# Low parts of the weights: all 861 subtractions on VectorE, and the MLP's second square on ScalarE

## The chip, the core and the metric

The kernel runs on one core of a Trainium2 chip. The metric is device microseconds of one execution. Engines are named as in the profile: PE is TensorE (PEld its weight loads), DVE is VectorE, ACT is ScalarE, POOL is GpSimd, SP is SyncE.

## What is computed

A forward pass of 256 tokens of width 1024 through two blocks of two layers each, in float32. The first block has latent attention, memory cross attention, an MLP, stick-breaking attention, again cross attention and an MLP. The second has retention, a layer of experts, sparse attention (nsa) and a second layer of experts, with scales and shifts from a conditioning vector (adaLN). What matters here:

```python
def sq_relu_mlp(h, w_in, w_out):
    return jnp.square(jax.nn.relu(h @ w_in)) @ w_out

def peer(h, w_q, sub_keys, u_tab, v_tab):
    ...
        s = jnp.einsum('thcd,hcnd->thcn', q, sub_keys, preferred_element_type=f32)
        sv, si = lax.top_k(s, PEER_TOPK)
    ...
        cv, ci = lax.top_k(comb, PEER_TOPK)
    ...
        w = jax.nn.softmax(cv, axis=-1)
        u = u_tab[eidx]
        a = jax.nn.gelu(jnp.einsum('td,thkd->thk', xc, u, preferred_element_type=f32)) * w
        return jnp.einsum('thk,thkd->td', a.astype(v_tab.dtype), v_tab[eidx])
```

The tables u and v hold 16384 experts. The kernel doesn't gather them: it multiplies with all of them and weights the result by masks.

## The kernel before

**Weights in two parts.** Every product is made of three: high part times high part, and the two mixed products with the low parts, all in float32r. The weights come as a stream of 861 granules of 128 x 1024 float32 (512 KB), in the order of use. For each granule SP loads `raw`, ACT copies it rounded to float32r into `wh` (L279), and a subtraction makes `wl` = `raw` - `wh` (L285). There are four buffers of each. A granule serves 24 matmuls of 256 columns or 12 of 512.

**The order around it.** Nothing is scheduled by a tool; each engine runs what the program issues, in that order. `block()` hands out the weights. At the first block of a granule it runs one step of each background generator (`tick`), then `ahead()`, then the posts. `ahead()` first issues the subtraction of the granule cast one granule earlier, and with it the load that refills its raw buffer, then casts the granule three places further on. So a low part is issued two granules before its use. In `_conv` the engine of the subtraction is chosen by a counter:

```python
        eng = k.nc.gpsimd if k.pool_share and (g + 1) % k.pool_share == 0 else k.nc.vector
```

With `pool_share` 2 every second granule goes to POOL, with 1 each, with 3 each third, with 0 none; it is 2 for most stages and is set anew around some of them. At 1 it stands where DVE builds masks.

**The MLP** (`mlp`, L1087 to L1114). Each of the 32 tiles of the hidden layer takes one granule. Behind it ACT makes z = relu (L1100) and the high part of z squared (L1101), DVE squares z again in full float32 (L1102) and subtracts (L1103). Through these stages the adaLN vector is made in the background: of every three steps of `ada_gen` two issue a load of 512 KB and a DVE reduction of 128 x 1024 (L697).

**The expert layers** (`peer`). While PE makes queries and the first products with u, DVE searches the 16 largest scores of 32 rows, later of 16 more (`top16`, L1504 to L1512). The generator `route` takes two searches where the cast counter is even and one where it is odd (L1551). Then masks are made: L1607 on DVE, L1611 on POOL, sums L1618 and L1619 on DVE. Each product tile of u is added up by DVE (L1683). In four stages `w_gen` weights the hidden values by masks E, A and B on DVE (L1700, L1702, L1705), which PE multiplies (L1713), and DVE scales (L1720). The products with v (L1769) take their operand from a split whose low part gl is made on DVE (L555).

**Other work named.** A split (L557, L558) makes high and low halves of an operand (`x`, `raw`, `m`); sums of squares are added up on POOL (L349).

Of the kernel before, what the change touches and what calls it, by code (L numbers as in the profile page):

```python
# [19 lines left out]
S = 256  # L20
# [27 lines left out]
# ---------------------------------------------------------------- host layout  # L48


def _tiles(w, cols):
    """Blocks [128, 128] of w[K, N] for the column tiles in cols, K innermost."""
    k = w.shape[0] // P
    out = []
    for c in cols:
        t = w[:, c].reshape(k, P, P)
        out.append(t)
    return np.concatenate(out, axis=0)


def _grans(blocks):
    """[n, 128, c] blocks to granules [g, 128, 1024]."""
# [8 lines left out]
def _pack_t(w, cols=None, group=0):  # L71
    """Column tiles one after another; the first group of them block by block in turn."""
# [10 lines left out]
def _pack_v(w, width=512):  # L83
    """Blocks [128, width], column group outermost, K innermost."""
    k, n = w.shape[0] // P, w.shape[1] // width
    b = w.reshape(k, P, n, width).transpose(2, 0, 1, 3).reshape(n * k, P, width)
    return _grans(b)


def _feat(v):  # L90
    """[..., n * 128] vectors to columns [128, ...]."""
    return np.ascontiguousarray(v).reshape(-1, P).T
# [47 lines left out]
def _rope_cols():  # L140
    """Per row of the table: frequency, phase, phase in turns."""
# [101 lines left out]
# ---------------------------------------------------------------- weight stream  # L243


class Stream:
    """Weights in order of use: loaded ahead, then split into a float32r part and its rest."""
# [25 lines left out]
    def _conv(self):  # L273
# [6 lines left out]
        eng = k.nc.gpsimd if k.pool_share and (g + 1) % k.pool_share == 0 else k.nc.vector  # L280
# [3 lines left out]
        def rest():  # L284
            eng.tensor_tensor(l, raw, h.bitcast(F32), op=ALU.subtract)  # L285
# [9 lines left out]
    def ahead(self):  # L295
        """Casts go AHEAD granules in front, their rests one turn later, when the cast is done."""
# [30 lines left out]
# ---------------------------------------------------------------- kernel body  # L327


class TileSum:  # L330
    """Sums over the features of n tiles: all but the last add up on another engine, then ones times both."""
# [34 lines left out]
class Kern:  # L366
    def __init__(self, tc, aps, ctx):
# [6 lines left out]
        self.pool_share = 2  # L374
        self.mk, self.mst, self.mv = [], [], []

    # -- helpers
# [15 lines left out]
    def logexp(self):  # L393
        """Ln and Exp from one table set."""
        self.nc.scalar.preload_act_table_set("natural_log_exp_and_others")

    def post(self, f):
        """Run f, which waits for another engine, behind what can go first."""
        self.posts.append(f)
# [6 lines left out]
    def later(self, f, tiles=1):  # L406
        """Run f, work for the tensor engine, so many product tiles later."""
        self.defer.append([tiles, f])

    def due(self, cap=3):  # L410
        """What to run behind the tile that starts now."""
# [27 lines left out]
    def pair(self, pool, name, kts=KT):  # L439
        """Tiles of an operand and of its rest, side by side: both, and the two as one."""  # L440
# [3 lines left out]
    def lin_head(self, name, xh, xl, kt, evac, psum, tag, pre=None, look=5, hook=None, banks=None, ahead=False):  # L444
        """The first GROUP tiles of a product at once, so that each operand tile serves them all when it comes.
        banks: one for each, for operands wider than S."""
# [39 lines left out]
    def lin_t(self, name, xh, xl, kt, nt, evac, psum=None, tag="lin", first=0, mid=32, hook=None, hl=None):  # L486
        """out^T tiles [128, S] of (x @ w): weights stationary.
        hl: the operand and its rest side by side, for tiles that take both with one load of the weights; the last tile doesn't."""
# [30 lines left out]
    def lin_v(self, name, xh, xl, kt, cg, evac, pre=None, look=3, mid=KT, hook=None):  # L519
        """out tiles [128 tokens, 512] of (x @ w): activations stationary."""  # L520
# [28 lines left out]
    def split(self, h, l, src, scale=None):  # L549
        """h + l = src (* scale per partition), both float32r."""  # L550
# [9 lines left out]
    def rstd(self, ps, n, eps, pool, name, width=S, out=None):  # L560
        """(ps / n + eps) ** -0.5 with one Newton step."""
# [26 lines left out]
    # -- setup  # L588
# [16 lines left out]
    def early_load(self, u):  # L605
        """The rest of the first loads, between the first units of weights."""
# [18 lines left out]
    def bank(self, kind, shape):  # L625
        """A bank for short use: in turn from those of all kinds, or from its own kind's."""
# [12 lines left out]
    def rope_table(self, room):  # L639
        """Rows of cosines, then sines with the signs that the swapped halves take."""  # L640
# [27 lines left out]
    def silu_c(self):  # L668
        """c / (1 + exp(-c)), by exponentials and a logarithm"""
# [13 lines left out]
    def ada_gen(self):  # L683
        """mod[:, j] = sum_k silu(c)[k] * w[k, j * 128 + p] + bias, one tile of features per step."""
# [22 lines left out]
    # -- residual stream with an RMS norm ahead  # L707

    def norm_begin(self, gname, gi, kts=KT, tag="x", pool=None, bank="sum"):
        """Operands of x * g; the norm's factor per token comes later from finish()."""  # L710
# [19 lines left out]
    def resid(self, name, oh, ol, kt, nxt, scale=None, pre=None, hl=None):  # L730
        """X += o @ w, tile by tile, with the next norm's operands."""
# [17 lines left out]
        if pre:  # L749
            share, self.pool_share = self.pool_share, 1 if kt < KT else self.pool_share  # L750
            self.lin_head(name, oh, ol, kt, evac, self.ps, "lin", pre=pre, look=1)
            self.pool_share = share
        self.lin_t(name, oh, ol, kt, KT, evac, first=GROUP if pre else 0, hl=hl)

    def late(self, st, n, name, flush=True):
        """The norm's factor, worked out behind the first product that uses the operands."""
# [8 lines left out]
    # -- softmax attention  # L765

    def soft_causal(self, ps, scale, pool, sb=3):
        """Rows of [q0 x k0 | q1 x (k0, k1)] in ps; exponentials and their sums, for soft_norm."""
# [38 lines left out]
    def pv(self, pT, v0, v1):  # L807
        """o^T [dv, q] from [k0 x (q0, q1) | k1 x q1]."""
# [6 lines left out]
    class Pipe:  # L815
        """Steps of heads; step i + 1 of a head comes lag[i] turns after step i."""
# [24 lines left out]
        def pre(self, every, head=lambda e: e):  # L841
            """Hook of lin_head: the heads left over come out while the products that need them last go on."""
# [12 lines left out]
    # -- block 1  # L855

    def mla(self):
# [3 lines left out]
        with tc.tile_pool(name="mla", bufs=1, reuse_waits="tile") as mp:  # L861
# [19 lines left out]
            def lat_norms(n):  # L881
                """Factors of the two inner norms on top of the outer one."""
# [26 lines left out]
            share, self.pool_share = self.pool_share, 3  # L909
            self.lin_head("mla_dkv", st["h"], st["l"], KT, evac, self.ps, "lin", pre=pre, look=KT)  # L910
            self.pool_share = share
# [1313 lines left out]
```

## Time and profile before

| what | value |
|---|---|
| median of 3 runs | 3097.62 us |
| the runs | 3095.78, 3097.62, 3098.09 us |
| span of the profiled execution | 3094.6 us, 46975 instructions |
| time of the profiled execution itself | not given apart from its span; the runs lie 1.2 to 3.5 us above the span, the median 3.0 |
| PE / DVE / ACT / POOL busy | 94% / 72% / 47% / 48% |
| subtractions on POOL / on DVE | 496 / 365 |

Busy time is the union of an engine's instructions; the mean of a group is over its single durations, which overlap slightly where instructions follow each other. "Idle before" names what ended the idle time of an engine. A wait is put down to the releaser that came last.

### The profile page before, as it was taken

The numbers are of one execution on the slowest core, as the hardware profiler recorded it, in microseconds if no ns is written. First come the engines' busy times: TensorE is split into PE (matmuls) and PEld (weight loads), VectorE is DVE, ScalarE is ACT, GpSimd is POOL, SyncE is SP. The second block draws the span as 40 slices with busy tenths as digits, with TensorE's granted clock in tenths as the row PEclk, the third lists the DMA queues.
The fourth block names the chain that finished last, engine by engine and source line by source line (L and its number), as shares of the span: only waits on it lengthen the run. The fifth ranks groups of instructions, "written<-read, shape, count | busy, mean of one in ns | idle before, by whom it ended". The sixth has DMA issues, their size and how long they took to land.

```text
span 3094.6 us, 46975 instructions
## 1 busy us (share of the span) xinstructions
PE 2920.4 (94%) x17758; PEld 2566.3 (83%) x17758; DVE 2218.5 (72%) x3966; ACT 1467.0 (47%) x2347; POOL 1500.5 (48%) x758
## 2 busy tenths in 40 slices
PE   7898999889999899999999999788999999999998
PEld 6888888888988887898888888677988898888886
DVE  6869986799768898676547666787897773367434
ACT  6455444553544555434542344565555334532444
POOL 4344456435555556454444444423566444455443
PEclk9999999999999999999999999999999999999999
DMA  5547775477554455434653356332455335643463
GB/s 180 197 152 253 283 271 207 164 266 287 183 177 130 146 182 166 145 112 140 188 170 109 123 188 188 117 110 77 157 184 177 124 113 171 186 145 114 150 188 119
DMA packets 143408, 521.06 MB, mean 168 GB/s; under 512 B 15919, under 2 KB 17229, under 8 KB 142669
## 3 DMA queue, kind: packets, MB, share of 16 engines
q1 hardware_dynamic: 142893, 515.96, 50.4%
q8 instruction: 139, 2.28, 0.3%
q10 hardware_dynamic: 288, 2.10, 0.2%
q14 instruction: 88, 0.72, 0.1%
HBM read 516.95 MB, written 1.05 MB: 167 GB/s over the span
## 4 chain that ended last, share of the span: by engine, by line
PE 64%; DVE 24%; issue 5%; POOL 3%; ACT 3%; DMA 1%; SPq 0%; DVEq 0%; ACTq 0%; POOLq 0%
PE vo L1769 22%; PE u L1675 11%; PE w L1713 8%; PE u L1676 6%; DVE wl L285 5%; DVE adaw L697 2%; PE lin L499 2%; PE lin L437 2%; PE lin L435 2%; DVE y L1102 2%; PE lin L436 2%; POOL wl L285 1%; PE lin L500 1%; POOL oh L1611 1%; PE lin L539 1%
## 5 line engine op out<-in xcount | busy, mean ns | idle before, releaser
L285 POOL TENSOR_TENSOR wl<-raw,wh 128x1024 fp32r<-128x1024 f32 x496 | 1248.1, 2518 | 1350.6 <-ACT wh L279 1340.5
L279 ACT ACTIVATE wh<-raw 128x1024 fp32r<-128x1024 f32 x861 | 910.3, 1058 | 650.6 <-PE vo L1769 331.6
L1675 PE MATMUL u<-x,wh 128*128 128x512 f32 x2048 | 731.8, 400 | 0.0
L285 DVE TENSOR_TENSOR wl<-raw,wh 128x1024 fp32r<-128x1024 f32 x365 | 557.1, 1527 | 227.7 <-ACT wh L279 227.5
L1676 PE MATMUL u<-x,wl 128*128 128x256 f32 x2048 | 577.5, 282 | 16.7 <-POOL wl L285 8.5
L1675 PEld LDWEIGHTS u<-x,wh 128*128 128x128 f32 x2048 | 387.8, 189 | 87.6
L1676 PEld LDWEIGHTS u<-x,wl 128*128 128x128 f32 x2048 | 389.0, 190 | 23.8 <-POOL wl L285 12.0
L1769 PE MATMUL vo<-wh,gh 128*128 128x512 f32 x1008 | 322.3, 401 | 0.0
L1769 PE MATMUL vo<-wh,gl 128*128 128x512 f32 x1008 | 316.3, 395 | 0.0
L1769 PE MATMUL vo<-wl,gh 128*128 128x512 f32 x1008 | 316.1, 395 | 0.0
L437 PE MATMUL lin<-x,wl 128*128 128x256 f32 x920 | 267.9, 291 | 24.3 <-DVE wl L285 22.3
L1713 PE MATMUL w<-B,A 128*128 128x64 f16 x2048 | 274.6, 303 | 9.7 <-DVE B L1705 9.5
L435 PE MATMUL lin<-x,wh 128*128 128x256 f32 x920 | 274.1, 298 | 3.3 <-DVE cq L558 2.8
L1713 PEld LDWEIGHTS <-A 128*128 128x128 f16 x2048 | 240.6, 147 | 38.2 <-DVE A L1702 19.9
L436 PE MATMUL lin<-x,wh 128*128 128x256 f32 x920 | 264.7, 288 | 3.6 <-DVE x L558 3.6
L1680 ACT COPY G<-u 128x256 f32<-128x256 f32 x256 | 94.8, 370 | 335.7 <-PE u L1676 335.1
L555 DVE TENSOR_TENSOR gl<-G,gh 128x512 fp32r<-128x512 f32 x128 | 170.7, 1334 | 93.5 <-ACT gh L554 93.3
L1769 PEld LDWEIGHTS vo<-wl,gh 128*128 128x128 f32 x1008 | 190.2, 189 | 44.6
L1769 PEld LDWEIGHTS vo<-wh,gl 128*128 128x128 f32 x1008 | 190.1, 189 | 44.3
L1769 PEld LDWEIGHTS vo<-wh,gh 128*128 128x128 f32 x1008 | 186.7, 191 | 38.8
L1683 DVE TENSOR_TENSOR G<-u,G 128x256 f32<-128x256 f32 x256 | 106.4, 417 | 149.7 <-ACT G L1680 149.6
L437 PEld LDWEIGHTS lin<-x,wl 128*128 128x128 f32 x920 | 180.2, 196 | 31.3 <-DVE wl L285 28.1
(551 smaller groups left out, 5471.0 us busy)
## 6 DMA issues: line engine op xcount, KB each, us to landing
raw<-in_peer_u SPq DMA_DIRECT2D x256, 512.0 KB, 3.5
raw<-in_peer_v SPq DMA_DIRECT2D x256, 512.0 KB, 3.6
adaw<-in_ada SPq DMA_DIRECT2D x112, 512.0 KB, 5.2
raw<-in_mlp_in SPq DMA_DIRECT2D x64, 512.0 KB, 4.5
raw<-in_mlp_out SPq DMA_DIRECT2D x64, 512.0 KB, 5.0
raw<-in_peer_q SPq DMA_DIRECT2D x32, 512.0 KB, 3.5
raw<-in_sb_qk SPq DMA_DIRECT2D x16, 512.0 KB, 4.3
raw<-in_ret_g SPq DMA_DIRECT2D x16, 512.0 KB, 3.6
```

The lines of the kernel that those rows point to most:

```text
L279: k.nc.scalar.activation(h, raw, AF.Copy)
L285: eng.tensor_tensor(l, raw, h.bitcast(F32), op=ALU.subtract)
L435: mm(ps, wh, xh, start=start, stop=False)
L436: mm(ps, wh, xl, start=False, stop=False)
L437: mm(ps, wl, xh, start=False, stop=stop)
L555: self.post(lambda: vec.tensor_tensor(l, src, h.bitcast(F32), op=ALU.subtract))
L1675: mm(p, wh, hx[:, i], start=i == 0, stop=False, skip_group_check=True)
L1676: mm(p[:, 0, :], wl, hh[:, i, :], start=False, stop=i == KT - 1, skip_group_check=True)
L1680: nc.scalar.copy(g, p[:, 1, :])
L1683: nc.vector.tensor_tensor(g, p[:, 0, :], g, op=ALU.add)
L1713: mm(pt[:, t, :], A[:, :, t], B[:, j, :, t], start=j == 0, stop=j == 1)
L1769: mm(vo[2 * b + e], x[:, j, t], w[:, e * 512:(e + 1) * 512], start=fst and m == 0, stop=bool(lst) and m == 2)
```

## The change

All subtractions are issued on DVE, and `pool_share` with every place that sets it is gone. In the MLP, the full square of z is made by ACT, by a Square activation. Comments and doc strings are gone as well, which shifts the line numbers (L285 is L284 after, L1683 is L1676).

```diff
@@ -277,12 +277,11 @@
         k.nc.scalar.activation(h, raw, AF.Copy)
-        eng = k.nc.gpsimd if k.pool_share and (g + 1) % k.pool_share == 0 else k.nc.vector
         self.conv[g] = (h, l)
         self.next_conv += 1

         def rest():
-            eng.tensor_tensor(l, raw, h.bitcast(F32), op=ALU.subtract)
+            k.nc.vector.tensor_tensor(l, raw, h.bitcast(F32), op=ALU.subtract)
             if self.next_dma < len(self.grans):
                 self._dma()
...
@@ -1099,7 +1093,7 @@
                 nc.scalar.activation(z, p, AF.Relu)
                 nc.scalar.activation(yh[:, n, :], z, AF.Square)
-                nc.vector.tensor_tensor(y, z, z, op=ALU.mult)
+                nc.scalar.activation(y, z, AF.Square)
                 nc.vector.tensor_tensor(yl[:, n, :], y, yh[:, n, :].bitcast(F32), op=ALU.subtract)
...
@@ -1817,24 +1809,19 @@
         LATE = PART - EARLY
         late = G0[:, LATE:, :]
-        self.pool_share = 1
         self.bg.append(w_gen(0, [(G0, PART, 0)], lambda: prep("a", G0)))
```

What it moves on DVE, at three places. The rows are the program's order; they hold no time. `ISA adaw,mod` is the adaLN reduction and `ISA mod` the read of its sum.

First, DVE in the first MLP, over three tiles. Before:

```order
L697 ISA adaw,mod<-adaw,crow 128x1024
L697 ISA mod 128x1
L285 TENSOR_TENSOR wl<-raw,wh 128x1024
L1102 TENSOR_TENSOR y<-z 128x256
L1103 TENSOR_TENSOR y_2276<-y,y_2276 128x256
L1102 TENSOR_TENSOR y<-z 128x256
L1103 TENSOR_TENSOR y_2276<-y,y_2276 128x256
L697 ISA adaw,mod<-adaw,crow 128x1024
L697 ISA mod 128x1
L285 TENSOR_TENSOR wl<-raw,wh 128x1024
L1102 TENSOR_TENSOR y<-z 128x256
L1103 TENSOR_TENSOR y_2276<-y,y_2276 128x256
```

After:

```order
L695 ISA adaw,mod<-adaw,crow 128x1024
L695 ISA mod 128x1
L284 TENSOR_TENSOR wl<-raw,wh 128x1024
L1097 TENSOR_TENSOR y_2276<-y,y_2276 128x256
L284 TENSOR_TENSOR wl<-raw,wh 128x1024
L1097 TENSOR_TENSOR y_2276<-y,y_2276 128x256
L695 ISA adaw,mod<-adaw,crow 128x1024
L695 ISA mod 128x1
L284 TENSOR_TENSOR wl<-raw,wh 128x1024
L1097 TENSOR_TENSOR y_2276<-y,y_2276 128x256
```

Every tile now has a subtraction in DVE's queue, and none a square.

Second, DVE in the routing of the second expert layer, over one round of two granules (`G` holds the scores and the hidden values). Before:

```order
L285 TENSOR_TENSOR wl<-raw,wh 128x1024
L1683 TENSOR_TENSOR G_21557<-u,G_21557 128x256
L1504 MAX sv_21585<-G_21557 128x8 x2
L1506 MAX_INDEX si_21586<-sv_21585,G_21557 128x8 x2
L1508 MATCH_REPLACE G_21557<-sv_21585,G_21557 128x128 x2
L1510 MAX sv_21585<-G_21557 128x8 x2
L1512 MAX_INDEX si_21586<-sv_21585,G_21557 128x8 x2
L1683 TENSOR_TENSOR G_21557<-u,G_21557 128x256
L1504 MAX sv_21585<-G_21557 128x8
```

After:

```order
L284 TENSOR_TENSOR wl<-raw,wh 128x1024
L1676 TENSOR_TENSOR G_21557<-u,G_21557 128x256
L1498 MAX sv_21585<-G_21557 128x8 x2
L1500 MAX_INDEX si_21586<-sv_21585,G_21557 128x8 x2
L1502 MATCH_REPLACE G_21557<-sv_21585,G_21557 128x128 x2
L1504 MAX sv_21585<-G_21557 128x8 x2
L1506 MAX_INDEX si_21586<-sv_21585,G_21557 128x8 x2
L284 TENSOR_TENSOR wl<-raw,wh 128x1024
L1676 TENSOR_TENSOR G_21557<-u,G_21557 128x256
L1498 MAX sv_21585<-G_21557 128x8
```

The double search, which shared its granule with a POOL subtraction, now has one behind it on DVE.

Third, DVE under the masks of the first expert layer, one step. Before:

```order
L1720 SCALAR_TENSOR_TENSOR G_10625<-w,G_10625 128x64x8
L1700 TENSOR_TENSOR E<-iota_1190,i2T 128x512
L1702 TENSOR_TENSOR A<-iota_1190,i1T 128x1024
L1705 TENSOR_TENSOR B<-E,wT 128x512 x2
L1683 TENSOR_TENSOR G_13341<-u,G_13341 128x256
```

After:

```order
L1713 SCALAR_TENSOR_TENSOR G_10625<-w,G_10625 128x64x8
L1693 TENSOR_TENSOR E<-iota_1190,i2T 128x512
L1695 TENSOR_TENSOR A<-iota_1190,i1T 128x1024
L1698 TENSOR_TENSOR B<-E,wT 128x512 x2
L284 TENSOR_TENSOR wl<-raw,wh 128x1024
L1676 TENSOR_TENSOR G_13341<-u,G_13341 128x256
```

Here no subtraction stood on DVE before, and now one stands in each step, behind the masks.

## Rows read from the trace of the kernel before

**Rows 1.** The page's first part: busy time, share and instructions of each engine.

```profile
PE 2920.4 (94%) x17758; PEld 2566.3 (83%) x17758; DVE 2218.5 (72%) x3966; ACT 1467.0 (47%) x2347; POOL 1500.5 (48%) x758
```

**Rows 2.** Chain that ended last, in order: start us, us, what (products with v).

```profile
1761.56 178.46 PE vo L1769 x768
```

**Rows 3.** List of waits: engine line waited for, us in total, times, longest.

```profile
PEld lin L437 <- DVE wl L285: 30.1, 31, 3.0
...
PEld u L1676 <- POOL wl L285: 12.0, 11, 2.2
...
PEld u L1676 <- DVE wl L285: 11.7, 11, 1.4
...
PE w L1713 <- DVE B L1705: 9.5, 5, 3.9
...
PEld w L474 <- DVE raw L558: 8.4, 7, 2.5
...
PEld lin L500 <- DVE wl L285: 7.5, 6, 2.1
...
PEld lin L437 <- POOL wl L285: 7.4, 9, 1.6
```

**Rows 4.** Groups: operation, count, then busy us, mean ns, idle before.

```profile
L285 POOL TENSOR_TENSOR wl<-raw,wh 128x1024 fp32r<-128x1024 f32 x496 | 1248.1, 2518 | 1350.6 <-ACT wh L279 1340.5 <-DVE kl L1432 8.0 <-issue 1.6
...
L285 DVE TENSOR_TENSOR wl<-raw,wh 128x1024 fp32r<-128x1024 f32 x365 | 557.1, 1527 | 227.7 <-ACT wh L279 227.5
...
L1700 DVE TENSOR_TENSOR E<-iota,i2T 128x512 f16<-128x512 f16 x128 | 172.9, 1351 | 0.1
L555 DVE TENSOR_TENSOR gl<-G,gh 128x512 fp32r<-128x512 f32 x128 | 170.7, 1334 | 93.5 <-ACT gh L554 93.3
...
L1102 DVE TENSOR_TENSOR y<-z 128x256 f32<-128x256 f32 x64 | 70.8, 1107 | 0.7 <-ACT z L1100 0.6
...
L1101 ACT ACTIVATE y<-z 128x256 fp32r<-128x256 f32 x64 | 26.7, 418 | 2.0
```

**Rows 5.** View of line L285: durations in ns, min/median/max, first and last start.

```profile
L285 DVE TENSOR_TENSOR wl<-raw,wh x365: 1201/1221/3430, 5.4 to 3065.5; 128x1024 fp32r<-128x1024 f32 x183
```

**Rows 6.** Timeline of POOL and DVE, first MLP: start us, us, instruction.

```profile
260.47 2.73 POOL L285 TENSOR_TENSOR wl<-raw,wh 128x1024 fp32r<-128x1024 f32 x1 [4.96 <-ACT wh L279]
...
260.86 2.62 DVE L1102 TENSOR_TENSOR y<-z 128x256 f32<-128x256 f32 x1
...
263.93 1.22 DVE L285 TENSOR_TENSOR wl<-raw,wh 128x1024 fp32r<-128x1024 f32 x1
265.07 0.42 DVE L1102 TENSOR_TENSOR y<-z 128x256 f32<-128x256 f32 x1
```

**Rows 7.** Timeline of POOL and DVE, start of the first masks.

```profile
1274.32 5.82 POOL L285 TENSOR_TENSOR wl<-raw,wh 128x1024 fp32r<-128x1024 f32 x2 [4.36 <-ACT wh L279]
...
1277.82 2.87 DVE L1702 TENSOR_TENSOR A<-iota,i1T 128x1024 f16<-128x1024 f16 x1
...
1284.36 0.41 DVE L1700 TENSOR_TENSOR E<-iota,i2T 128x512 f16<-128x512 f16 x1
```

**Rows 8.** Stretches: us, busy us (xinstructions) of PE, PEld, DVE, ACT, POOL, clock, DMA share, GB/s.

```profile
220.00:320.00 100.00, 90.42 (x713) 87.72 (x712) 95.28 (x116) 53.36 (x92) 38.82 (x15) 0.98 0.73 258
1300.00:1450.00 150.00, 150.00 (x967) 133.71 (x966) 108.31 (x169) 53.91 (x82) 75.39 (x32) 1.00 0.36 117
2218.00:2300.00 82.00, 82.00 (x481) 72.47 (x480) 80.03 (x335) 48.64 (x75) 55.43 (x28) 1.00 0.63 199
```

**Rows 9.** The same view: one round of routing in layer 0, one in layer 1.

```profile
1092.85:1099.84 6.99, 5.91 (x34) 4.89 (x33) 6.85 (x29) 3.07 (x5) 2.39 (x2) 1.00 0.44 154
2242.50:2248.40 5.90, 5.90 (x36) 5.20 (x36) 5.76 (x29) 3.13 (x6) 3.14 (x1) 1.00 0.57 175
```

**Rows 10.** Timeline of DVE, start of that round in layer 0.

```profile
1092.85 2.36 DVE L285 TENSOR_TENSOR wl<-raw,wh 128x1024 fp32r<-128x1024 f32 x1
```

**Rows 11.** Waits of PE's weight loads, 1075 to 1160 us.

```profile
PEld u L1676 <- DVE wl L285: 7.2, 6, 1.4
```

More of the change, by code (lines that the diff above doesn't have):

```diff
@@ L373, in __init__ @@
         self.ada, self.quiet = None, False
-        self.pool_share = 2
         self.mk, self.mst, self.mv = [], [], []
@@ L749, in resid @@
         if pre:
-            share, self.pool_share = self.pool_share, 1 if kt < KT else self.pool_share
             self.lin_head(name, oh, ol, kt, evac, self.ps, "lin", pre=pre, look=1)
-            self.pool_share = share
         self.lin_t(name, oh, ol, kt, KT, evac, first=GROUP if pre else 0, hl=hl)
@@ L907, in pre @@
                 self.norm_tile(st, i, self.X[:, i, :])
-            share, self.pool_share = self.pool_share, 3
             self.lin_head("mla_dkv", st["h"], st["l"], KT, evac, self.ps, "lin", pre=pre, look=KT)
-            self.pool_share = share
             self.lin_t("mla_dkv", st["h"], st["l"], KT, 6, evac, first=GROUP)
@@ L1653, in peer @@
         self.bg.append(route())
-        share, self.pool_share = self.pool_share, SHARE
         banks = []
@@ L1774, in v_end @@
             gh, gl = sp.pop((key, c))
-            self.pool_share = 0
             w = [self.ws.block(f"peer_v{layer}", D, hold=j > 0) for j in range(2)]
@@ L1823, in peer @@
         assert not self.bg
-        self.pool_share = share
         v_chunks("a", G0, LATE, nxt=("b", late), first=True)
         u_chunks(PART + EARLY, 2 * PART, G0, (pu,))
-        self.pool_share = 1
         self.bg.append(w_gen(1, [(G1, EARLY, 0), (G0, LATE, EARLY)], lambda: prep("c", G1)))
@@ L1830, in peer @@
         assert not self.bg
-        self.pool_share = share
         self.logexp()
@@ L1836, in peer @@
         self.ln_stats(3 if layer else 0)
-        self.pool_share = share
         es.close()
@@ L1848, in nsa @@
             w2 = mp.tile([P, 2, 256], F32, name="w2")
-            share = self.pool_share
             nat = mp.tile([P, 4, S], F32, name="nat")
@@ L1915, in nsa @@
             self.lin_head("nsa_k", R[:, :, 0], R[:, :, 1], KT, ev, None, None, pre=self.raw_pre, look=2, hook=clear, banks=banks)
-            self.pool_share = 1
             self.lin_t("nsa_k", R[:, :, 0], R[:, :, 1], KT, 8, ev, first=GROUP)
@@ L1925, in run @@
                         f()
-            self.pool_share = 2
             self.lin_v("nsa_v", kh, kl, KT, 1, evac_v, hook=run)
-            self.pool_share = 0
             GN = NSA_G * CMP_N
@@ L1985, in second @@
                     nc.vector.tensor_tensor(vc[:, i, :], p, half, op=ALU.mult)
-            self.pool_share = share
             self.lin_t("nsa_gate", h1[0], h1[1], KT, 1, evac_g)
```

## The prediction

> **What bounds the kernel now.** I read the page's first part first: TensorE (PE) is busy 94% of the span, VectorE (DVE) 72%, ScalarE 47%, GpSimd (POOL) 48% [rows 1]. PE is the bound, so the change can pay only where PE stands still, or cost where it makes PE stand still. How much that can be, the chain says: in the long products of the expert stage 768 matmuls take 178.46 us [rows 2], that is 64 granules of weights (12 matmuls of 512 columns each) at 2.79 us. A granule of 24 matmuls of 256 columns has as many columns, so I price it the same.
>
> Next the list of waits, filtered to what holds PE or its weight loads [rows 3]. The loads wait for the low parts wl: 30.1 + 7.5 + 7.4 us in the ordinary products, 12.0 + 11.7 us in the expert products; 68.7 us in all. Beside them stand 9.5 us in which PE waits for the masks B and, in the largest group of its kind, 8.4 us in which loads wait for the operand halves raw. These three kinds, some 87 us, are what this change can reach.
>
> Why is wl late? The group view shows 496 subtractions on POOL of 2518 ns and 365 on DVE of 1527 ns [rows 4], while the view by source line gives DVE a median of 1221 ns [rows 5]. The timeline of the first MLP shows what lifts DVE's mean: POOL starts a subtraction at 260.47 us that runs 2.73 us; DVE's square (L1102) starts at 260.86 and needs 2.62 us, the next one, with POOL quiet, 0.42 us [rows 6]. So while POOL runs a subtraction, DVE operations that read two SBUF operands stand until it ends, and everything behind them in DVE's queue with them. At the start of an expert stage two POOL subtractions (5.82 us) stretch the mask A to 2.87 us; the next mask E takes 0.41 us [rows 7], against its mean of 1351 ns [rows 4].
>
> **The change, part by part.** *The 496 subtractions.* POOL loses 496 x 2.5 = 1249 us. DVE gains 496 operations; two that follow each other start 1.14 us apart (263.93 to 265.07) [rows 6], so 496 x 1.14 = 565 us. In return the standing ends: (1527 - 1221) x 365 = 112 us on wl itself, (1351 - 410) x 128 = 120 us on E, (1334 - 680) x 128 = 84 us on gl [rows 4]; the 680 is an estimate for 512 elements between 1221 ns for 1024 [rows 5] and 420 for 256 [rows 6]. The squares leave with 71 us. That is 387 us from four groups, and smaller groups (the adaLN rows, A, x, raw) may add 100. DVE thus goes from 2218 us to about 2300 us: nearly a wash, but with no foreign lock in it. What matters is where.
>
> *In the two MLPs.* Of every three granules two carry an adaLN row (1024 elements, so 1.14 us by pace), and each ends with L1103. Before, DVE was busy 95.28 of 100 us [rows 8], and 713 matmuls are 29.7 granules, so one took 3.37 us. After, three granules ask of DVE 3 x 1.14 + 3 x 0.43 (L1103 free of the lock, the length of a 256-element op as in [rows 6]) + 2 x 1.14 = 7.0 us, and of PE 3 x 2.79 = 8.4 us. PE becomes the bound there and its waits for wl go. Each subtraction is written one granule after its cast and two before its use, 5.6 us of cover; the longest piece in front of it now, L1103 and an adaLN row, is 1.6 us. Of the 30.1 + 7.5 us I take 35. The 7.4 us behind POOL: 6.
>
> *The second square.* DVE loses 64 operations, ScalarE gains 64 of about 418 ns, the mean of L1101, which already squares the same tile [rows 4]. ScalarE is busy 53.36 of those 100 us [rows 8]; 29.7 tiles x 0.42 = 12.5 us more do not fill it. L1101 stands between the same neighbours today, so no other function comes in. Its cost on the path: the next cast starts 0.4 us later, with three granules of cover; L1103 now waits for ScalarE instead of DVE. I take nothing, and 64 x 0.42 = 27 us as the far bound, if every tile's cover were gone.
>
> *DMA and queues.* The refill of a raw buffer is issued by SyncE behind its subtraction; that ends 1.2 us sooner by its own length. No DMA is added. In the MLPs the transfers must speed up with the product: a granule and two thirds of an adaLN row are 0.87 MB per 2.9 us, 301 GB/s, where they ran 258 GB/s at a share of 0.73 [rows 8], so 353 GB/s at a full share by estimate. Free, but see the third rival.
>
> *Start of the expert stages.* A took 2.87 us under the lock and E is 0.41 us without it [rows 7]; E, A and B stand in one row on DVE ahead of PE's first product, and each loses some 2 us of standing. The 9.5 us of waits for B go: 9.
>
> *Operand halves.* The low half of raw reads two SBUF tiles of 256 elements, so it is held as the square is (2.62 against 0.42 us) [rows 6]. Of the 8.4 us I take half, 4, and as much again at x and m, which are made the same way: 8; bounds 0 and 17. POOL's own remaining work (sums of squares, masks) no longer stands behind subtractions: 4, bounds 0 and 9.
>
> *Routing, where it can cost.* Here DVE finds the 16 largest of each row while PE runs expert products. In layer 0 one round of two granules takes 6.99 us with DVE busy 6.85 of it [rows 9]; PE wants only 2 x 2.79 = 5.58 [rows 2]. One held subtraction of 2.36 us [rows 10] is shortened by 1.14 and one of 1.14 is added: unchanged, so the 7.2 us that loads wait for DVE's wl there [rows 11] stay. In layer 1 the round happens to miss the lock: its round takes 5.90 us, DVE busy 5.76, the subtraction not held [rows 9]. With 1.14 more it becomes 7.0 against PE's 5.58. Over the 82 us of this stretch, with DVE busy 80.03 [rows 8] and 15 subtractions more (17 us), DVE asks 97 less some held time; it may fall up to 15 us behind, of which 5.6 us of cover, refilled once between the two rounds of search, save a good part. Bounds 0 and 15; I take 6, and 3 for the second round of layer 0. What follows is the gather of indices, where POOL's multiplies alternate with subtractions and loads wait 12.0 us for POOL's wl and 11.7 - 7.2 = 4.5 us for DVE's [rows 3, 11]. The multiplies remain and still hold DVE's subtractions, so of 16.5 us I take 10.
>
> *Weighting by masks.* All subtractions ran on POOL here: 150 us with DVE at 108.31 [rows 8]. 30 more (75.39 / 2.518) cost 34 us, E gives back 30 x 0.94 = 28: 114 of 150. Nothing; DVE keeps 36 us free, and if E were not sped up it would still keep 8.
>
> Sum: 35 + 6 + 9 + 8 + 4 + 10 - 6 - 3 = 63 us. The profiled span is 3094.6 us, the median of the runs 3097.6, 3.0 outside it. 3094.6 - 63 + 3.0 = **3035 us**.
>
> *A rule against it.* The rows show a DVE busy 95 of 100 us in the MLP and 80 of 82 in the routing [rows 8]. The Trainium skill (Perfetto Trace Analysis, Optimizing Scalar/DVE Operations) says that a saturated DVE may be a reason to give work to ScalarE or even GpSimd, the opposite of this change. By the busy rows taken at face value the sum is the fourth rival's; by the 0.42 beside the 2.62 [rows 6] much of that busy time is standing, and the sum is mine. The same section adds that shifting work between DVE and GpSimd might not help since they share a port; that fits the rows, and would make the change small rather than large.
>
> **The rivals.**
> 1. *DVE's queue takes POOL's place* (chance 0.14). A subtraction now stands behind DVE operations that wait for PE or ScalarE, which POOL's did not. For it: the routing rounds are full [rows 9]. Against: 5.6 us of cover. If half of 35 + 6 + 10 comes back and the routing costs its full 15 in both layers: 3035 + 26 + 21 = 3082 us.
> 2. *No change* (0.04). PE finds another wait behind each one removed (the second operand, the evacuation): 3097 us, within 0.2% (6.2 us), about what a measurement of this kernel can tell from no change.
> 3. *Transfers bound the MLPs* (0.06). At 301 GB/s loads land later and the casts wait. If half the MLP gain is lost: 3035 + 18 = 3053 us.
> 4. *DVE is saturated* (0.06), the slower side. Its busy time is work, and the added 1.14 us per moved subtraction comes on top wherever it is over nine tenths busy. In the MLPs' second products (64 granules, 64 x 2.9 = 186 us) no square leaves, and 17 us per 100 (15 subtractions) come on top of a DVE that I take to be as busy as before: 112 of 100, 22 us. In routing 97 of 82 us in layer 1 and the same in layer 0: 30 us. The gains are absent: 3097.6 + 52 = 3150 us. It decides once DVE asks more than 2.79 us per granule in a whole product outside routing.
>
> That the change does not do what it says is excluded by the order: no subtraction is left on POOL.
>
> **How the numbers follow.** The forecast has 0.70, its own spread from the bounds: all 87 us gone and POOL's 4, no cost: 3007, so I begin at 3005; routing at 15 + 9, 15 more than taken, and a fifth of the 72 us of gains missing: 3064. The range takes in rivals 1 and 3 and leaves out rivals 2 and 4: 3005 to 3082. Faster by over 0.2%: 0.70 + 0.14 + 0.06 = 0.90; same 0.04; slower 0.06.
>
> **What would show it.** Right: 861 subtractions on DVE at about 1.22 us mean, L1700 near 0.41, DVE busy near 2300 us; loads waiting for wl under 25 us, nearly all in the routing stages; a tile of the first MLP every 2.8 to 2.9 us; the routing round of layer 1 at 7.0 us. Wrong: waits for wl in MLP or under masks, ScalarE's casts waiting for raw transfers there, or the stretch from 2218 us in layer 1 over 15 us longer.

## The result, and the profile after

The changed kernel takes 2983.59 us (median of 4 runs, 2978.25 to 2984.76), the kernel before 3096.70 us beside it (4 runs, 3095.12 to 3098.09): a ratio of 0.9634, interval 0.9621 to 0.9648, 113 us gained. Forecast were 3035 us and a range that began at 3005: the direction was right, the size was not, and the range was too high. The profiled execution of the changed kernel took 2984.09 us, its span is 2982.4 us.

The page's first part after, against [rows 1]:

```profile
PE 2889.5 (97%) x17758; PEld 2551.4 (86%) x17758; DVE 2247.6 (75%) x4398; ACT 1485.1 (50%) x2411; POOL 272.1 (9%) x262
```

PE ran the same 17758 matmuls. It stood still for 3094.6 - 2920.4 = 174 us before and for 2982.4 - 2889.5 = 93 us after: 81 of the 112 us of span are standing that went, and 31 are matmuls that took less time. DVE, which took over 496 subtractions, is busy only 29 us longer.

Groups after (line, operation, count, then busy us, mean ns, idle before), against [rows 4, 5]:

```profile
L284 DVE TENSOR_TENSOR wl<-raw,wh 128x1024 fp32r<-128x1024 f32 x861 | 1084.6, 1263 | 315.0 <-ACT wh L279 314.4
...
L553 DVE TENSOR_TENSOR gl<-G,gh 128x512 fp32r<-128x512 f32 x128 | 87.6, 684 | 0.0
...
L1693 DVE TENSOR_TENSOR E<-iota,i2T 128x512 f16<-128x512 f16 x128 | 53.2, 416 | 0.0
```

A DVE subtraction is at 1263 ns where it was at 1527, E at 416 where it was at 1351, gl at 684 where it was at 1334. Forecast were about 1220, 410 and an estimate of 680.

Waits after (what waited, for what: us, times, longest), against [rows 3]:

```profile
PEld u L1669 <- DVE wl L284: 25.5, 36, 1.6
...
PE u L1669 <- DVE wl L284: 13.1, 17, 1.3
...
PEld w L472 <- DVE raw L556: 3.1, 2, 1.6
...
PEld lin L435 <- DVE wl L284: 1.3, 1, 1.3
```

In the ordinary products the wait for wl is gone but for 1.3 us (30.1 before), that of w for raw fell from 8.4 to 3.1 us, the 9.5 us that PE stood behind B no longer stand in the list (the loads wait for B more often now, 62 times and 0.3 us at most, and the matmuls behind them not at all). What grew is the wait of u's loads for DVE's wl, 11.7 to 25.5 us. But before they also waited 12.0 us for POOL's wl [rows 3], so all their waits for wl went from 23.7 to 25.5 us: in the searches of the routing from 7.2 [rows 11] to 18.0 us, from their end on from 16.5 down to 7.5 us. A load's wait is not yet PE's: the second row shows the matmuls' own waits, 13.1 us, and they lie inside the 25.5 us.

The table that the prediction lacked is the view of stretches over the whole program. PE alone: stretch, its length, busy us (matmuls), clock as a share of full speed, DMA share, GB/s. Before:

```profile
0.00:220.00 220.00, 184.74 (x1254) 0.98 0.50 172
220.00:412.00 192.00, 177.21 (x1203) 0.98 0.75 268
412.00:605.00 193.00, 175.84 (x1213) 0.97 0.58 205
605.00:790.00 185.00, 173.18 (x1191) 0.99 0.74 265
790.00:1010.00 220.00, 212.16 (x1459) 0.99 0.50 163
1010.00:1940.00 930.00, 903.80 (x5041) 0.99 0.48 154
1940.00:2160.00 220.00, 184.50 (x1284) 0.96 0.31 98
2160.00:3094.60 934.60, 909.00 (x5125) 0.99 0.48 152
```

The same pieces of the program after, cut at the same matmuls to within four:

```profile
0.00:204.00 204.00, 181.35 (x1255) 0.99 0.55 187
204.00:373.00 169.00, 169.00 (x1200) 1.00 0.88 311
373.00:549.00 176.00, 168.32 (x1216) 0.99 0.63 216
549.00:716.00 167.00, 167.00 (x1187) 1.00 0.84 297
716.00:931.00 215.00, 209.45 (x1463) 1.00 0.51 167
931.00:1845.00 914.00, 902.03 (x5039) 1.00 0.49 157
1845.00:2047.00 202.00, 180.99 (x1284) 0.97 0.33 107
2047.00:2982.40 935.40, 911.32 (x5125) 0.99 0.47 152
```

The second and fourth line are the MLPs: 377 us became 336, with PE busy all the time. The sixth and eighth are the expert layers: 1864.6 became 1849.4. The first, third, fifth and seventh are everything else (attentions, retention): 853 became 797. The prediction names the 6 us behind POOL among the MLPs and the 4 us of raw among the operand halves in general; the list of waits, taken piece by piece, puts the 7.4 us behind POOL into the first and third piece (3.0 and 4.3 us) and the 8.4 us of w for raw into the expert layers (4.4 and 4.0 us), so they are counted there:

| pieces | forecast gain, us | measured | of it standing of PE | of it shorter matmuls |
|---|---|---|---|---|
| MLPs | 35 | 41 | 27 | 14 |
| expert layers | 9 + 10 - 6 - 3 + 4 = 14 | 15 | 16 | -1 |
| the other stages | 6 + 4 + 4 = 14 | 56 | 39 | 17 |

So two of three rows came out within 6 us, and the third was missed by 42. Standing is a piece's length less PE's busy time.

### The profile page after: what moved, and what is told of

Its sections match the earlier page's. It is cut to its first block, busy times and chain, and to the rows that moved or that the text cites. A ratio compares the mean times of both kernels' runs of the same rounds, so it can differ in the third digit from the quotient of the medians.

```text
span 2982.4 us, 46836 instructions
## 1 busy us (share of the span) xinstructions
PE 2889.5 (97%) x17758; PEld 2551.4 (86%) x17758; DVE 2247.6 (75%) x4398; ACT 1485.1 (50%) x2411; POOL 272.1 (9%) x262
## 4 chain that ended last, share of the span: by engine, by line
PE 77%; DVE 18%; issue 2%; ACT 2%; DMA 0%; POOL 0%; SPq 0%; DVEq 0%; ACTq 0%; POOLq 0%
PE vo L1762 24%; PE u L1668 10%; PE w L1706 9%; DVE wl L284 6%; PE u L1669 5%; PE lin L434 4%; PE lin L433 4%; PE lin L435 4%; PE lin L497 4%; PE lin L498 2%; PE lin L537 1%; PE lin L538 1%; PE lin L536 1%; DVE G L1676 1%; PE lin L472 1%
## 5 line engine op out<-in xcount | busy, mean ns | idle before, releaser
L284 DVE TENSOR_TENSOR wl<-raw,wh 128x1024 fp32r<-128x1024 f32 x861 | 1084.6, 1263 | 315.0 <-ACT wh L279 314.4
L1669 PE MATMUL u<-x,wl 128*128 128x256 f32 x2048 | 578.7, 283 | 14.4 <-DVE wl L284 13.1
L1669 PEld LDWEIGHTS u<-x,wl 128*128 128x128 f32 x2048 | 387.7, 189 | 25.9 <-DVE wl L284 25.5
L433 PE MATMUL lin<-x,wh 128*128 128x256 f32 x920 | 270.8, 294 | 2.3 <-ACT x L555 1.5
L1706 PEld LDWEIGHTS <-A 128*128 128x128 f16 x2048 | 240.1, 147 | 27.8 <-DVE B L1698 16.5
L434 PE MATMUL lin<-x,wh 128*128 128x256 f32 x920 | 262.0, 285 | 1.1 <-DVE x L556 0.9
L435 PE MATMUL lin<-x,wl 128*128 128x256 f32 x920 | 261.2, 284 | 0.0
L1713 DVE SCALAR_TENSOR_TENSOR G<-w,G 128x272 f32<-128x272 f32 (+1 forms) x192 | 92.5, 510 | 129.3 <-PE w L1706 129.3
L348 POOL TENSOR_TENSOR acc<-sq 128x256 f32<-128x256 f32 x17 | 15.4, 904 | 1833.2 <-ACT sq L337 1833.2
L433 PEld LDWEIGHTS lin<-x,wh 128*128 128x128 f32 x920 | 177.1, 192 | 4.2 <-ACT x L555 1.9
L434 PEld LDWEIGHTS lin<-x,wh 128*128 128x128 f32 x920 | 177.1, 193 | 3.0 <-DVE x L556 1.9
```

The costliest lines, as they stand in the source:

```text
L284: k.nc.vector.tensor_tensor(l, raw, h.bitcast(F32), op=ALU.subtract)
L433: mm(ps, wh, xh, start=start, stop=False)
L434: mm(ps, wh, xl, start=False, stop=False)
L435: mm(ps, wl, xh, start=False, stop=stop)
L1669: mm(p[:, 0, :], wl, hh[:, i, :], start=False, stop=i == KT - 1, skip_group_check=True)
L1706: mm(pt[:, t, :], A[:, :, t], B[:, j, :, t], start=j == 0, stop=j == 1)
```

## The experiments

Theory A: while GpSimd reads SBUF for a subtraction, a DVE operation with two SBUF operands stands, and with it all that is behind it in DVE's queue, whatever name PE's wait then bears. Rivals: GpSimd's own late work (its queue), the later return of `raw` (loads), or the square.

**What is it about GpSimd's subtraction that costs?** Three kernels keep all subtractions on DVE and give GpSimd something else to do at the 496 old places. The first reads SBUF and writes `raw`, when DVE is done with it:

```diff
+        also = k.pool_share and (g + 1) % k.pool_share == 0
...
+        def extra():
+            k.nc.gpsimd.tensor_tensor(raw, h.bitcast(F32), h.bitcast(F32), op=ALU.subtract)
...
+            k.nc.vector.tensor_tensor(l, raw, h.bitcast(F32), op=ALU.subtract)
+            if also:
+                extra()
```

> All 861 subtractions stay on VectorE, the square on ScalarE. At the 496 places where GpSimd subtracted before, GpSimd now runs a subtraction of the same size whose result nobody uses (the high part less itself, into the raw buffer after VectorE has read it). Theory A (the time was lost because GpSimd's reading holds VectorE's two-operand operations, and whatever stands behind them): the gain goes and more, since VectorE now also has 565 us of subtractions: 3090 to 3170 us. Theory B (the time was lost because GpSimd delivered the low parts late): the low parts still come from VectorE, so 2984 to 2995 us. Theory C (GpSimd's own sums and masks stood behind its subtractions): part of the gain goes, 2995 to 3030 us.

Measured: 3140.55 us (ratio to before 1.014, 1.0124 to 1.0157), 157 us above the changed kernel. The second writes the same tile and reads nothing:

```diff
+        def extra():
+            k.nc.gpsimd.memset(raw, 0.0)
+            k.nc.gpsimd.memset(raw, 0.0)
```

> The same kernel, but GpSimd's extra work is two memsets of the same raw buffer: it writes and reads nothing. Theory A: VectorE isn't held by an operation that reads nothing, 2984 to 3000 us. Theory B: 2984 to 2995 us. Theory C, and any cost of a busy GpSimd or of raw buffers that come free later: the same as the run with the reading operation, as far as the memsets last as long.

Measured: 3013.22 us (0.9727, 0.9711 to 0.9744), 30 us above it and 13 above what theory A allowed. The third keeps GpSimd's queue full behind the cast, and of DVE's operands reads one column of wh:

```diff
+        def extra():
+            t = k.stream.tile([P, 96], F32, name="pq", bufs=1)
+            k.nc.gpsimd.tensor_copy(t[:, 0:1], h.bitcast(F32)[:, 0:1])
+            for _ in range(14):
+                k.nc.gpsimd.memset(t, 0.0)
```

> The changed kernel, and at the 496 old places GpSimd, behind the cast, copies one column of wh and then fills a small tile of its own 14 times (96 columns each), about as long as its subtraction was; it reads one element per partition of SBUF and holds neither raw nor VectorE's operands. Theory A1 (of the 30 us that the writes into raw cost, most came from GpSimd's own work, masks and sums, that stood behind them in its queue): 3000 to 3015 us. Theory A2 (they came from raw being given back later, and loads with it): 2983 to 2992 us. If even so VectorE were held, E's mean would be near 1350 ns again and the time above 3040 us.

Measured: 2990.42 us (0.9646, 0.9629 to 0.9663), 7 us above it, with intervals that overlap. Groups of the three kernels, in this order:

```profile
L288 DVE TENSOR_TENSOR wl<-raw,wh 128x1024 fp32r<-128x1024 f32 x861 | 1234.6, 1438 | 228.2 <-ACT wh L279 227.9
L285 POOL TENSOR_TENSOR raw<-wh 128x1024 f32<-128x1024 f32 x496 | 1014.8, 2046 | 1702.5 <-DVE wl L288 1437.9 <-issue 75.3 <-ACT ss L784 27.0
...
L1705 DVE TENSOR_TENSOR E<-iota,i2T 128x512 f16<-128x512 f16 x128 | 170.0, 1328 | 0.0
```

```profile
L285 POOL MEMSET raw<- 128x1024 f32 x496 | 473.7, 955 | 1641.4 <-DVE wl L289 1330.7 <-issue 82.9 <-ACT wh L279 76.0
...
L1706 DVE TENSOR_TENSOR E<-iota,i2T 128x512 f16<-128x512 f16 x128 | 53.3, 417 | 0.0
```

```profile
L288 POOL MEMSET pq<- 128x96 f32 x6944 | 1240.5, 179 | 400.5
...
L1708 DVE TENSOR_TENSOR E<-iota,i2T 128x512 f16<-128x512 f16 x128 | 53.2, 415 | 0.0
```

The reads alone bring E back to 1328 ns, and 3140.55 - 3013.22 = 127 us with it; two memsets of 955 ns leave it at 417. In the third kernel GpSimd is busy 60% of the span, more than before the change (48%), and E is at 415 ns. The rule of the Trainium skill (SBUF — State Buffer, Who interferes with whom) that a VectorE instruction with two SBUF inputs contends with a GpSimd instruction that reads SBUF, and not with one that only writes it, agrees with these rows. The rivals are not thereby gone. The three kernels and the one before, cut at the start of the same matmuls in the profiled executions, differ from the changed kernel piece by piece (us; two kernels that do the same in a piece agree there within 4 us):

| pieces | before | reads (first) | writes (second) | full queue (third) |
|---|---|---|---|---|
| latent and first cross attention | 16 | 16 | 1 | -2 |
| stick-breaking and second cross attention | 17 | 27 | 11 | 13 |
| retention | 7 | 15 | 6 | 1 |
| sparse attention | 18 | 23 | 6 | 7 |
| MLPs | 40 | 35 | 0 | -2 |
| expert layers | 14 | 40 | 3 | -12 |

In the latent attention and the MLPs nothing costs but the reads. In the stick-breaking and the sparse attention a full queue on GpSimd alone, with DVE not held, brings back 13 of 17 and 7 of 18 us; the 7 us of the whole kernel are small because the expert layers ran 12 us faster with it, for a cause that stays open. Over the four other stages that is 19 of 58 us by this cut; the second kernel costs 24 there. The third kernel's queue is longer than the old one (60% against 48%), and the column that it reads keeps wh back (ScalarE's casts waited 349 us for that), so what GpSimd's own late work was worth in these stages is about a third by these two kernels; the other 34 to 39 us go with the subtractions that read. Beside these GpSimd's own masks z took longer too (mean 1150 ns before, 654 after, 359 in the third kernel), which no run holds apart. The stick-breaking attention in the third kernel (stretch, its length, busy us of PE, matmuls, clock, DMA share, GB/s):

```profile
370.00:559.00 189.00, 173.96 (x1215) 0.97 0.59 201
```

Waits there (us, times, longest) of ScalarE in the kernel before, the changed one and the third, and one of PE in the third:

```profile
ACT z L1172 <- POOL z L1170: 37.7, 8, 6.2
...
ACT z L1166 <- POOL z L1164: 21.2, 7, 4.6
...
ACT z L1180 <- POOL z L1178: 40.6, 7, 6.3
...
PE lin L546 <- DVE qk L1198: 3.1, 1, 3.1
```

ScalarE waits for masks z that GpSimd makes, and with a full queue it waits as long as before the change. The later return of `raw` is left with what the second kernel costs beyond the third, 23 us, most of it in the expert layers, where the third was the fast one; ScalarE's casts waited 54.1 us for loads of the MLPs' second weights in the second kernel and 8.2 in the changed one, but the MLPs are no slower for it, and it wasn't tried alone.

**The square.** Undone in the changed kernel, and done alone in the kernel before:

```diff
-                nc.scalar.activation(y, z, AF.Square)
+                nc.vector.tensor_tensor(y, z, z, op=ALU.mult)
```

> The changed kernel with the MLP's second square back on VectorE. Forecast of the prediction's step (the square is worth nothing by itself once nothing holds VectorE, which then asks 8.0 of 8.4 us in three MLP granules): 2981 to 2989 us. Rival (VectorE is the bound in the MLPs, so each square of 0.34 to 0.42 us counts): 64 of them, 3005 to 3011 us.

```diff
-                nc.vector.tensor_tensor(y, z, z, op=ALU.mult)
+                nc.scalar.activation(y, z, AF.Square)
```

> The kernel before with the square moved to ScalarE and nothing else. If VectorE in the MLPs is held by GpSimd, a square that leaves only passes the standing on to the next two-operand operation, but its own 0.42 us each is saved where VectorE bounds: 3070 to 3092 us. Rival (the square was the operation that caught the lock, 44 us of it over all tiles): 3050 to 3065 us. No change: 3094 to 3099 us.

Measured: 2983.72 us (0.9630, 0.9614 to 0.9646) with the square back, the changed kernel's 2983.59 for all that can be told; 3074.59 us (0.9925, 0.9907 to 0.9942) with the square alone, 23 us of gain. Where GpSimd still subtracts, a square on DVE is a held operation in a full queue; where it doesn't, it is 0.42 us beside the 2.8 us that a granule takes PE.

**Where the gain lies.** GpSimd's share as before (with every place that sets it) for some weights only, all else as in the changed kernel. The first leaves out MLPs and experts, as here; the second takes only the names of the MLPs, the third only those of the experts:

```diff
-            k.nc.vector.tensor_tensor(l, raw, h.bitcast(F32), op=ALU.subtract)
+            eng = k.nc.gpsimd if self.names[g][:3] not in ("mlp", "pee") and k.pool_share and (g + 1) % k.pool_share == 0 else k.nc.vector
+            eng.tensor_tensor(l, raw, h.bitcast(F32), op=ALU.subtract)
```

> The changed kernel, with GpSimd's share of the subtractions as before for the weights of the attentions, the retention and the other stages that are neither MLP nor experts; MLPs and experts keep all on VectorE. Theory A (what was held in VectorE's queue was all its work in these stages, the operand halves, softmax and evacuations too, whatever name the wait bore): the stages up to 220, 412 to 605, 790 to 1075 and 1940 to 2160 us lost 67 us from the kernel with the square alone to the changed one, so the time comes to some 3050 us (3035 to 3060). Theory B (only the waits that bore the names wl and raw, as the prediction counted): 18 to 27 us, so 3002 to 3011 us.

> The changed kernel, with GpSimd's share as before for the weights of the two MLPs alone; the square stays on ScalarE. Theory A: the stretches of the MLPs lost 20 us from the kernel with the square alone to the changed one, so some 3004 us (2998 to 3014). Theory B (the MLPs carry most of the gain, as the prediction had it, 35 of 63 us): 3015 to 3025 us.

> The changed kernel, with GpSimd's share as before for the weights of the two expert layers alone (queries, u and v). Theory A: these stretches differ by 4 us in all between the kernel with the square alone and the changed one, gains of 20 at the masks against losses of 16 in the searches, so some 2988 us (2980 to 2996). Theory B (gains of 9 for B and 10 for the gather of indices, losses of 9 in the routing): 2994 us.

Measured: 3040.80 us (0.9821, 0.9804 to 0.9837), 2999.99 us (0.9687, 0.9670 to 0.9703) and 2997.26 us (0.9675, 0.9656 to 0.9694). GpSimd's group in each, in this order:

```profile
L285 POOL TENSOR_TENSOR wl<-raw,wh 128x1024 fp32r<-128x1024 f32 x90 | 228.8, 2543 | 310.2 <-ACT wh L279 300.3 <-DVE kl L1432 8.0 <-issue 1.6
```

```profile
L285 POOL TENSOR_TENSOR wl<-raw,wh 128x1024 fp32r<-128x1024 f32 x66 | 191.2, 2904 | 124.1 <-ACT wh L279 124.1
```

```profile
L285 POOL TENSOR_TENSOR wl<-raw,wh 128x1024 fp32r<-128x1024 f32 x340 | 836.3, 2460 | 896.8 <-ACT wh L279 896.8
```

90 subtractions in the attentions and the retention cost 57 us (0.64 us each), 66 in the MLPs 16 us, 340 in the expert layers 14 us (0.04 us each). With the 23 us of the square alone that makes 110 of the 113 us. For the other stages theory A had 3035 to 3060 us and the prediction's way of counting 3002 to 3011, for the MLPs 2998 to 3014 and 3015 to 3025: A's figures hold in both. That tells where the subtractions cost, not how: in the other stages this run does not part a held DVE from GpSimd's own late work, as the table above does. For the expert layers the time lies just above A's 2980 to 2996 and 3 us from the other way's 2994, which parts nothing; in their masks and gathers GpSimd's subtractions still cost, and in their searches they help, as the next runs show.

**Back to GpSimd only where it pays.** A flag was to send every second subtraction to GpSimd while the searches run:

```diff
+            eng = k.nc.gpsimd if k.search and g % 2 else k.nc.vector
...
                 if now:
+                    self.search = True
                     top16(*now)
```

> The changed kernel, but while the searches for the 16 largest run, in both expert layers, GpSimd takes every second subtraction again (odd granules). Theory A (in the searches VectorE has more work than a tile of u lasts, and its rows hold few operations that GpSimd can hold): the waits of TensorE for wl in u, 38 us of which 23 lie in the searches, fall below 20 us, and the time by 6 to 18 us, to 2966 to 2978 us. Rival (a held subtraction on VectorE gives back what the other one saved): no change, 2980 to 2987 us.

Measured: 3005.04 us (0.9712, 0.9694 to 0.9730), slower than the changed kernel. The edit did not do what it was meant to: the second search of a layer raised the flag again, and it stayed up until the next layer's search or the end, so 282 subtractions went to GpSimd, from 953 us on. The next three lower it behind the second search, for both layers, for layer 1 alone, and for both with the even granules:

```diff
             while route_at[0] < 32:
+                self.search = bool(work)
                 route_at[0] += some(work)
                 yield
...
+            self.search = False
             ix = []
```

> The changed kernel, but GpSimd takes every second subtraction (odd granules) from the first row searched to the last, in both expert layers, and none after that. Theory A (in the searches VectorE has more work than a tile of u lasts): the waits of u for wl fall by some 9 us in layer 1 and by 3 us in layer 0, so 2972 us (2966 to 2979). Rival (what GpSimd holds there costs as much as it takes over): 2981 to 2987 us.

> The same for layer 1 alone. Theory A: the waits of u for wl in layer 1's searches, some 9 us, go, so 2975 us (2970 to 2980). Rival: 2981 to 2987 us.

> As the run for both layers, with the even granules instead of the odd ones: GpSimd's subtraction then stands beside the other step of the search (one row against two). Theory A, if the place in the step doesn't matter: as with the odd granules, 2966 to 2979 us. Rival (VectorE's late step is the one with two rows, and only the subtraction beside that counts): 2979 to 2987 us.

Measured: 2959.36 us (0.9553, 0.9539 to 0.9567), 2964.76 us (0.9569, 0.9555 to 0.9583) and 2968.12 us (0.9575, 0.9561 to 0.9589). The first beats both kernels: 24 us under the changed one, more than theory A's 5 to 18, with 36 subtractions on GpSimd. Its waits of u for wl, and GpSimd's group:

```profile
PEld u L1673 <- DVE wl L285: 7.5, 6, 1.5
...
PE u L1673 <- DVE wl L285: 5.6, 6, 1.2
```

```profile
L285 POOL TENSOR_TENSOR wl<-raw,wh 128x1024 fp32r<-128x1024 f32 x36 | 94.7, 2630 | 131.6 <-ACT wh L279 131.6
```

The loads' waits fell from 25.5 to 7.5 us and the matmuls' from 13.1 to 5.6. The first of these expectations added the two rows up, but they are the same waits seen at two engines: of the matmuls' 13.1 us 13.0 lie within the loads' waits. So 7.5 us of PE's standing behind wl account for a part of the 24 us; in the two profiled executions PE's standing fell by 11 us in all and its busy time by 11 (2889.5 to 2878.9), and where the rest comes from stays open. The waits behind the searches went too. The kernel for layer 1 alone can't be told from the one for both. With the even granules the rival (no gain beside the single search) falls; whether odd or even is better the overlapping intervals leave open.

## Why the prediction was wrong

The step that failed is the ceiling: "These three kinds, some 87 us, are what this change can reach." It added up waits of loads that bore the names wl, B and raw. Summed over PE's own waits in the two traces, those under these names fell from 80 to 21 us: 59 us, where the sum had 55 (35 + 6 + 9 + 4 + 10 - 6 - 3). The other 53 us were not in the ceiling: 22 us of standing under other names, and 31 us of shorter matmuls. The first lie in the attentions and the retention, where a held operation, or GpSimd's own work behind its subtractions, makes others late. Pieces of the chain of waits before, in the attention that follows the first MLP (start us, us, what):

```profile
416.82 3.41 DVE adaw L697
420.23 3.32 DVE wl L285
423.92 0.44 DVE X L742
...
425.24 0.48 DVE x L558
425.72 1.14 DVE adaw L697
...
489.77 2.52 POOL z L1170 x2
```

The adaLN row takes 3.41 us held and 1.14 free, the subtraction 3.32 against a median of 1221 ns [rows 5]; X and x, which PE wants, are short and late by what stands in front of them. The last line is GpSimd's own: two masks z, behind a subtraction in its queue. The list of waits before has such waits as lines of a few us each (us, times, longest):

```profile
PE lin L538 <- DVE rawb L1412: 5.5, 1, 5.5
...
PE t L797 <- DVE ss L790: 4.8, 4, 2.0
...
PE lin L538 <- DVE qk L1190: 3.2, 1, 3.2
```

In the sparse attention the wait for rawb is 2.0 us after the change and that for ss 1.2, and with GpSimd's queue full (third kernel) rawb is at 2.0 too and ss no longer in the list: these were a held DVE. The wait for qk is gone after the change, but back at 3.1 us in the third kernel, whose DVE is not held: it goes with GpSimd's queue, though DVE's name is on it. The sum priced all of this at 4 (x and m) and 4 (GpSimd's own work, bounds 0 and 9), where the third kernel's queue, with DVE not held, costs 19 us in these stages. The stretches would have shown that there was more: PE busy 757.2 of 853 us in these four pieces, so 96 us of standing, of which the sum touched 14. After it is 740.1 of 797, 57 us of standing.

A second term is missing from the sum altogether: what a wait does to PE's clock. Before, one stretch of the first MLP (length, busy, matmuls, clock, DMA share, GB/s):

```profile
326.00:329.00 3.00, 3.00 (x19) 1.00 0.86 347
329.00:332.30 3.30, 1.50 (x9) 1.00 0.99 377
333.00:336.00 3.00, 3.00 (x11) 0.50 0.82 280
```

PE's first matmul behind the wait, in the timeline before:

```profile
332.31 0.39 PE L500 MATMUL lin<-y,wl 128*128 128x256 f32 x1 [1.81 <-DVE wl L285]
```

PE waits 1.81 us for wl, and then runs at 0.50 of full speed (1.2 of 2.4 GHz) and starts 11 matmuls where it starts 19 at full speed. The mean granted clock rose from 0.987 to 0.994: (1 - 0.987) x 3094.6 = 40 us short of full speed before and 0.006 x 2982.4 = 18 us after. These 22 us are an estimate, and lie within the 31 us by which PE's busy time fell; the rest of the 31 stays open. They weren't tried apart, since no run removed the waits and kept the clock low, and that waits brought the clock down elsewhere too is argued from this one place.

Point by point:

- *The mechanism* (two SBUF operands stand while GpSimd reads) was right: 1263, 416 and 684 ns as forecast, DVE busy 2248 us against about 2300.
- *MLPs*, PE as the bound: right, and 41 us for 35. That the number is near is in part luck: the loads waited there for wl (33.4 us of the 37.6 priced), but PE stood only 27 us, and 14 us came from shorter matmuls, which no term held. A window with as many matmuls as the 100 us of [rows 8] takes 85.70 us, 2.88 us a granule (first row below), as said; DVE is down to 70.22 of it.
- *The square* at nothing: right for the changed kernel, but only because the subtractions moved too.
- *GpSimd's own work* at 4 us, bounds 0 and 9: too small, some 19 us in the attentions and the retention by the third kernel.
- *Routing* at -6 and -3, the gather behind it at 10: the loads' waits for wl grew by 10.8 us in the searches and fell by 9.0 behind them. The size in layer 1 was between the taken 6 and the bound of 15. The 82 us of [rows 8] became 93.30, and the round takes 6.98 us, 7.0 forecast (second and third row). Some 18 of the 25.5 us of waits for wl that were left could be had back by three dozen subtractions on GpSimd.

Stretches of the changed kernel (length, then busy us of PE, PEld, DVE, ACT, POOL, clock, DMA share, GB/s):

```profile
203.90:289.60 85.70, 85.70 (x714) 85.59 (x713) 70.22 (x105) 61.78 (x122) 0.00 (x0) 1.00 0.85 297
2105.00:2198.30 93.30, 87.05 (x481) 72.94 (x480) 91.05 (x350) 47.37 (x76) 5.68 (x4) 1.00 0.51 163
2121.48:2128.46 6.98, 6.18 (x34) 4.90 (x33) 6.84 (x30) 3.07 (x6) 0.00 (x0) 1.00 0.51 162
```

- *The rivals.* Transfers did not bind: 297 GB/s at a share of 0.85, and PE never idle. DVE's queue took GpSimd's place in the routing only. The saturated DVE of the fourth rival was standing, not work; the Trainium skill's advice to hand work of a saturated VectorE on (Perfetto Trace Analysis, Optimizing Scalar/DVE Operations) costs 113 us here when it is followed in all stages and gains 24 us in the searches alone; its caution in the same place, that moving work between the two might not help, is the milder form of what was measured. The searches' rows tell why they are the exception: their operations (MAX8, FIND_INDEX8, some 0.28 us each) last as long with GpSimd's reads beside them as without. FIND_INDEX8 before and after (durations in ns, min/median/max, first and last start):

```profile
L1506 DVE FIND_INDEX8 si<-sv,G x64: 278/284/289, 1039.7 to 2256.1; 128x8 uint32<-128x128 f32 x64
...
L1500 DVE FIND_INDEX8 si<-sv,G x64: 275/284/291, 958.1 to 2151.9; 128x8 uint32<-128x128 f32 x64
```

## What to carry to other kernels

When a change frees an engine's queue, don't take as its ceiling the waits that bear the names of what moves: everything behind a held operation is late under its own name, in the queues of both engines. Set beside them the standing of the bound engine in each stage (stretch less busy time). That is no ceiling either: the MLPs had 27 us of standing and gained 41, since the matmuls grew shorter too. Don't add a wait of the loads to the wait of the matmuls behind them. Put work on GpSimd by what VectorE runs at that moment: in the attentions and the retention 90 subtractions cost 57 us, beside searches 36 of them gained 24 us. And compare a control kernel stage by stage: the third kernel's few us in all were 19 lost in some stages and 14 gained in others. Before calling an engine saturated, compare one operation's time with the neighbour busy and quiet.

## What the hardware showed that was not expected

GpSimd's load as such does not lengthen VectorE's operations: 7440 instructions that write a tile of their own, 496 of which read one column, keep it busy 60% of the span and leave E at 415 ns, while 496 reading instructions of 2046 ns cost 127 us more than writes of the same tile without reads. And a wait of 1.81 us cost PE more than its length: in 3 us at the half clock behind it 11 matmuls started, where 19 did before it.
